# A hybrid trunk's FFN gate and up tiles by seven half-depth products instead of eight

## The chip, the cores and the metric

One program on one core of one Trainium2 chip. The metric is the time of one execution on the device in microseconds (us), lower is better. All arithmetic is fp32: each product is made of fp32 operands split in two parts for TensorE.

## The reference

Two layers are applied to 640 tokens of 1024 features: 128 tokens of a context stream and 512 of a sample stream, with the same weights and two different modulation vectors (shift, scale, gate). Each layer is an FFN, a token mixing and a second FFN:

```python
def swiglu(h, w_in, w_out):
    gate, up = jnp.split(h @ w_in, 2, axis=-1)
    return (jax.nn.silu(gate) * up) @ w_out
...
    mod = (jax.nn.silu(cond) @ lp['w_mod'] + lp['b_mod'])[:, None, :]
...
    x = x + 0.5 * g1 * swiglu(modulate(rmsnorm(x, nw[0]), sh1, sc1), lp['ffn_w_in'][0], lp['ffn_w_out'][0])
    y, s_ssd, s_ret, k, v = token_mixing(modulate(rmsnorm(x, nw[1]), sh2, sc2), lp, ssd_s0, ret_s0, ctx_kv)
    x = x + g2 * y
    x = x + 0.5 * g3 * swiglu(modulate(rmsnorm(x, nw[2]), sh3, sc3), lp['ffn_w_in'][1], lp['ffn_w_out'][1])
```

w_in is 1024 x 5632 (2816 gate columns, 2816 up columns), w_out 2816 x 1024, both different for each of the four FFNs. The token mixing projects to four groups of heads (state space, Hyena with long convolutions whose filters come from a small network, retention, attention) and back.

## The kernel before

Everything is feature-major: a tensor holds 128 features on the partitions and tokens along the columns. x is eight such tiles of 640 tokens, worked on in two groups of 320 columns (group 0 has the 128 context tokens and 192 of the sample's). A matmul takes a 128x128 piece of weights and 320 columns of activations; every product of weights w and activations h is three matmuls, w_hi*h_hi, w_hi*h_lo and w_lo*h_hi (`mm3`, lines 326 to 332), accumulated in PSUM.

*Weights.* `wload` (L317) loads up to 128x1024 into `raw` (two buffers, RB), ACT copies it to `hi`, DVE makes `lo` = raw - hi (L61). *Activations.* `norm` (L303) squares x on ACT, adds the squares over the feature tiles on POOL (`nsum`, L282; on DVE at the very start), sums over partitions by matmuls, takes the power -0.5 on POOL (`nrs`, L120), spreads the result by another matmul, scales x on DVE (`nx`, L70) and splits it into `hh` (ACT) and `hl` (DVE, 640 columns at a time). The shifts stand as two extra columns beside group 0 (`shifts`, L297), so that the products of group 0 have 322 columns and bring what the shifts add.

*FFN* (`ffn`, L348, four times). The 22 pairs of gate and up tiles of 128 columns each (a pair is called a gate/up tile, or a tile, below) run in chunks of 6, 5, 4, 4 and 3; after each chunk its part of the down projection is accumulated into x (`accumulate`, L342). For a pair, each group and each matrix is a product over eight depth tiles:

```python
 355              for ci, nk in enumerate(FFN_CHUNKS):
 356                  G = []
 357                  for f in range(ff, ff + nk):
 358                      wg, wu = (ahead[i] if 2 * f + i < len(ahead) else self.wload(I["ffnin"][li, w, 2 * f + i], 1024)
 359                                for i in range(2))
 360                      gh = self.ring("gh", 640, F32R)
 361                      gl = self.ring("gl", 640, F32R)
 362                      for g in range(2):
 363                          c = slice(320 * g, 320 * g + 320)
 364                          pg = self.unit(wg, g)
 365                          if g == 0:
 366                              cg = mp.tile([128, 2, 2], F32, tag="cg", name="cg", bufs=3)
 367                              self.ccopy(cg[:, 0], pg[:, 320:322])
 368                          t = mp.tile([128, 320], F32, tag="sg", name="sg", bufs=3)
 369                          for a, b, st in GCOLS[g]:
 370                              self.act(t[:, a:b], pg[:, a:b], AF.Silu, bias=cg[:, 0, st : st + 1])
 371                          pu = self.unit(wu, g)
 372                          if g == 0:
 373                              self.ccopy(cg[:, 1], pu[:, 320:322])
 374                          p = mp.tile([128, 320], F32, tag="gu", name="gu")
 375                          for a, b, st in GCOLS[g]:
 376                              self.stt(p[:, a:b], pu[:, a:b], cg[:, 1, st : st + 1], t[:, a:b], ADD, MUL)
 377                          self.acopy(gh[:, c], p)
 378                          self.tt(gl[:, c], p, gh[:, c].bitcast(F32), SUB)
 379                          credit += 2.0 if ci == 0 else rate
 380                          while credit >= 1.0:
 381                              next(mods, None)
 382                              credit -= 1.0
 383                      G.append([(gh[:, 320 * g : 320 * g + 320], gl[:, 320 * g : 320 * g + 320]) for g in range(2)])
```

`mods` are pieces of the modulation that later stages need, computed inside the FFNs: each piece reduces one 128x1024 weight tile against silu(cond) on DVE (`wmj`, L270). `credit` pulls four pieces per pair in the first chunk, then `rate` x 2 per pair (rates 1.5, 1, 1, 1), and one per output tile of the down projection. The four FFNs have 96, 64, 80 and 16 pieces to do.

*Order.* The program is written as above, and the framework's scheduler makes each engine's queue from it by its own estimates; an engine takes its queue in that order. Pieces of the modulation are pinned to the program's order. The Hyena filters of a layer (`filters`, L442; small matmuls with names mx, w, h, pm, tab_c) are written ahead of an FFN (the first and the third feed-forward) and mixed by the scheduler into its first matmuls. The names: mm is a product's PSUM tile, mx any other PSUM tile; PSUM has eight banks, three for mm and five for mx. `ring` buffers (NB = 22 of 128x640) hold x, the gate-times-up tiles `gh` and `gl` of a chunk, and the mixers' inputs.

In the trace the FFNs run from 52 to 540, 950 to 1450, 1462 to 1930 and 2340 to 2814 us; the mixers lie between the first and second, and the third and fourth.

## Time and profile before

| | |
|---|---|
| median of two runs | 2812.73 us (2810.97 and 2814.49) |
| the profiled execution: its time, its span | 2814.49 us, 2814.5 us |
| PE busy | 2751.3 us, 98% of the span, 18,470 instructions |
| DVE busy | 1678.3 us, 60% |
| ACT busy | 915.1 us, 33% |
| POOL busy | 123.7 us, 4% |

PE is TensorE, DVE VectorE, ACT ScalarE, POOL GpSimd. The granted clock of PE is given for a stretch as a share of its full speed. In time order a row gives the start, the length and, in brackets, the idle time before it with what ended it.

### The profile page before, as it was taken

To read this page: it belongs to the slowest core of one execution; us is meant where nothing else is said; L and a number is where in the kernel's file an instruction comes from. 1 tells how busy PE (TensorE), PEld (TensorE's weight loads), DVE (VectorE), ACT (ScalarE), POOL (GpSimd) and SP (SyncE) were. 2 spreads that over 40 slices of the span, in tenths; PEclk is the share of its full clock that TensorE was granted. 3 is DMA by queue.
4 is the path that set the end of the run, shared out by engine and by line. 5 is a ranking of instruction groups with operands and counts; after the bars stand their busy time and mean duration, and the time that the engine had idled before them with its cause. 6 is when DMAs were issued, how large, how long until landed. Compare 5 with 4: busy or idle time off the path is not lost.

```text
span 2814.5 us, 46104 instructions
## 1 busy us (share of the span) xinstructions
PE 2751.3 (98%) x18470; PEld 2661.3 (95%) x18470; DVE 1678.3 (60%) x3658; ACT 915.1 (33%) x1952; POOL 123.7 (4%) x201
## 2 busy tenths in 40 slices
PE   6999999999999999999999999999999999999999
PEld 4899999999999789999989999998999998999999
DVE  6685666566756767555457655656558577433433
ACT  3222222333555322222233222223245534222222
POOL 0000000200010200000020000002001012000000
PEclk9999999999999999999999999999999999999999
DMA  6353444322211244334214433443222123222222
GB/s 239 126 181 119 141 144 130 134 79 62 90 58 55 96 153 160 103 122 135 75 59 147 133 100 117 134 139 102 68 80 80 57 69 128 76 74 77 76 69 89
DMA packets 118289, 300.74 MB, mean 107 GB/s; under 512 B 19614, under 2 KB 42222, under 8 KB 117564
## 3 DMA queue, kind: packets, MB, share of 16 engines
q1 hardware_dynamic: 118076, 297.80, 33.3%
q8 instruction: 146, 2.39, 0.3%
q14 instruction: 67, 0.55, 0.1%
HBM read 283.55 MB, written 14.20 MB: 106 GB/s over the span
## 4 chain that ended last, share of the span: by engine, by line
PE 92%; DVE 3%; POOL 1%; DMA 1%; issue 1%; ACT 1%; SPq 0%; POOLq 0%; ACTq 0%; DVEq 0%
PE mm L88 81%; PE mx L88 10%; PE mx L93 2%; POOL nsum L282 1%; DVE nx L70 1%; DVE hl L61 0%; POOL nrs L120 0%; DVE x L70 0%; DVE lo L61 0%; DMA E<-cumd 0%; DMA wms<-in_wmod 0%; POOL arr L120 0%; ACT nsq L73 0%; DVE ndg L61 0%; DVE wmj L270 0%
## 5 line engine op out<-in xcount | busy, mean ns | idle before, releaser
L88 PE MATMUL mm<-hh,lo 128*128 128x320 f32 (+2 forms) x3936 | 1234.9, 314 | 4.9 <-DVE lo L61 4.9
L88 PE MATMUL mm<-hh,hi 128*128 128x320 f32 (+2 forms) x3936 | 1235.7, 314 | 2.8 <-ACT hi L76 1.4
L88 PE MATMUL mm<-hl,hi 128*128 128x320 f32 (+2 forms) x3936 | 1231.1, 313 | 4.3 <-DVE hl L61 4.3
L88 PEld LDWEIGHTS mm<-hl,hi 128*128 128x128 f32 (+1 forms) x3936 | 745.1, 189 | 15.1 <-issue 6.3
L88 PEld LDWEIGHTS mm<-hh,hi 128*128 128x128 f32 (+1 forms) x3936 | 745.5, 189 | 9.2 <-ACT hh L76 2.7
L88 PEld LDWEIGHTS mm<-hh,lo 128*128 128x128 f32 (+1 forms) x3936 | 742.6, 189 | 11.9 <-DVE lo L61 5.8
L76 ACT CAST hi<-raw 128x1024 fp32r<-128x1024 f32 (+3 forms) x390 | 359.7, 922 | 855.8 <-PE mm L88 813.9
L61 DVE TENSOR_TENSOR lo<-raw,hi 128x1024 fp32r<-128x1024 f32 (+3 forms) x390 | 415.2, 1065 | 234.0 <-ACT hi L76 233.2
L88 PE MATMUL mm<-gl,hi 128*128 128x320 f32 x1408 | 436.3, 310 | 0.0
L88 PE MATMUL mm<-gh,hi 128*128 128x320 f32 x1408 | 436.2, 310 | 0.0
L88 PE MATMUL mm<-gh,lo 128*128 128x320 f32 x1408 | 435.8, 310 | 0.0
L70 DVE SCALAR_TENSOR_TENSOR gu<-mm,cg,sg 128x128 f32<-128x128 f32 (+2 forms) x264 | 108.9, 437 | 410.3 <-ACT cg L76 286.2
L70 DVE SCALAR_TENSOR_TENSOR x<-mm,gate,x 128x128 f32<-128x128 f32 (+2 forms) x576 | 235.9, 435 | 189.9 <-PE mm L88 187.4
L270 DVE CUSTOM_DVE_ANT_0 wmj<-wm,condb 128x1024 bf16<-128x1024 f32 x264 | 321.6, 1218 | 11.4 <-DMA wm<-in_wmodT 6.1
L88 PEld LDWEIGHTS mm<-gl,hi 128*128 128x128 f32 x1408 | 265.4, 189 | 2.1 <-issue 2.1
L88 PEld LDWEIGHTS mm<-gh,hi 128*128 128x128 f32 x1408 | 265.5, 189 | 0.0
L88 PEld LDWEIGHTS mm<-gh,lo 128*128 128x128 f32 x1408 | 265.4, 189 | 0.0
L76 ACT COPY cg<-mm 128x2 f32<-128x2 f32 x176 | 28.0, 160 | 419.6 <-PE mm L88 419.4
L61 DVE TENSOR_TENSOR gl<-gu,gh 128x320 fp32r<-128x320 f32 x176 | 86.1, 489 | 41.8 <-ACT gh L76 41.8
L76 ACT CAST gh<-gu 128x320 fp32r<-128x320 f32 x176 | 80.8, 459 | 91.4 <-DVE gu L70 90.5
L73 ACT ACTIVATE sg<-mm,cg 128x128 f32<-128x128 f32 (+2 forms) x264 | 106.0, 436 | 2.8
L282 POOL TENSOR_TENSOR nsum<-nsum,nsq 128x320 f32<-128x320 f32 x70 | 64.5, 922 | 605.7 <-ACT nsq L73 603.5
(237 smaller groups left out, 1842.2 us busy)
## 6 DMA issues: line engine op xcount, KB each, us to landing
raw<-in_ffnin SPq DMA_DIRECT2D x176, 512.0 KB
wm<-in_wmodT SPq DMA_DIRECT2D x132, 512.0 KB
raw<-in_mixin SPq DMA_DIRECT2D x52, 512.0 KB
raw<-in_ffnoutA SPq DMA_DIRECT2D x64, 256.0 KB
raw<-in_ffnoutA SPq DMA_DIRECT2D x32, 384.0 KB
raw<-in_ffnoutA SPq DMA_DIRECT2D x32, 320.0 KB
wms<-in_wmod SPq DMA_DIRECT2D x12, 512.0 KB
raw<-in_ffnoutB SPq DMA_DIRECT2D x12, 512.0 KB
```

The lines of the kernel that those rows point to most:

```text
L61: self.nc.vector.tensor_tensor(out, a, b, op=op)
L70: self.nc.vector.scalar_tensor_tensor(out, a, s, b, op0=op0, op1=op1)
L73: self.nc.scalar.activation(out, in_, f, **k)
L76: self.nc.scalar.copy(out, in_)
L88: return self.nc.tensor.matmul(out, lhsT=lhsT, rhs=rhs, start=start, stop=stop)
L93: self.nc.tensor.transpose(out, in_, self.ident[b : b + n, b : b + n])
L270: return self.nc.vector.tensor_tensor_reduce(junk, raw, cb, 1.0, 0.0, op0=MUL, op1=ADD, accum_out=out)
L282: adder.tensor_tensor(s, s, sq, op=ADD)
```

## The change

Let A be the 2x2 blocks of weights of a pair (gate and up, each cut at half the depth: a11 and a12 of gate, a21 and a22 of up, 128x512 each) and B the 2x2 blocks of activations (depth halves by token groups). Instead of the eight block products, seven are made, after Strassen and Winograd: four of them from sums of weight blocks (`sa`, `sb`: four additions of 128x512 per pair, on POOL) and, for the activations, from sums of token blocks (factors T1 to T4, made once per FFN in `sums`, by DVE and ACT: `hr`, `hq`, split in `HX` for T1, and `th`/`tl` for T3, T2 and T4). Products that share a result accumulate in one PSUM tile; partial results are copied to SBUF by ACT (`cp`) and added by DVE.

```diff
-FFN_CHUNKS = (6, 5, 4, 4, 3)
+FFN_CHUNKS = (4, 4, 4, 4, 3, 3)
...
+    def normed(self, li, n, g, j, pb):
+        t = self.ring("hb").rearrange("p (a b) -> p a b", a=2)
+        for i in range(2):
+            m = j + 4 * i
+            self.tt(t[:, i], self.x[m][g], pb, MUL)
+            for a, b, st in GCOLS[g]:
+                self.act(t[:, i, a:b], t[:, i, a:b], AF.Identity, scale=self.sc[li][:, n, m, st : st + 1],
+                         bias=self.mod[li][:, 24 * n + m, st : st + 1])
+        return t
...
+    def norm(self, li, n, g, adder=None, pin=False):
+        pb = self.norm_stats(g, adder or self.nc.gpsimd, pin)
+        yield
+        kept = []
+        for j in range(4):
+            t = self.normed(li, n, g, j, pb)
+            if g == 0:
+                self.split(self.H0[0][:, j], self.H0[1][:, j], t)
+            else:
+                if n == 1:
+                    self.split(self.HX[0][:, j], self.HX[1][:, j], t[:, 0])
+                self.split(self.H3[0][:, j], self.H3[1][:, j], t[:, 1])
+                if n != 1:
+                    kept.append(t)
+                    if not pin:
+                        self.sums(j, t)
+        if pin and g:
+            yield
+            for j in range(4):
+                self.sums(j, kept[j])
+    def sums(self, j, t):
+        b = lambda p, i: self.H0[p][:, j, i].bitcast(F32)
+        q = self.ring("hq").rearrange("p (a b) -> p a b", a=2)
+        r = self.ring("hr").rearrange("p (a b) -> p a b", a=2)
+        self.tt(r[:, 0], t[:, 0], b(0, 0), SUB)
+        self.tt(r[:, 0], r[:, 0], b(1, 0), SUB)
+        self.tt(q[:, 0], t[:, 0], t[:, 1], SUB)
+        self.split(self.HX[0][:, j], self.HX[1][:, j], r[:, 0])
+        self.tt(q[:, 1], t[:, 1], r[:, 0], SUB)
+        self.split(self.T[0][:, j, 0:2], self.T[1][:, j, 0:2], q)
+        self.tt(r[:, 1], b(0, 1), q[:, 1], SUB)
+        self.tt(r[:, 1], r[:, 1], b(1, 1), ADD)
+        self.split(self.T[0][:, j, 2], self.T[1][:, j, 2], r[:, 1])
...
+    def product(self, ps, w, half, which, first, last):
+        for j, (h, l) in enumerate(self.factor(which)):
+            c = slice(512 * half + 128 * j, 512 * half + 128 * j + 128)
+            k = {} if first else {"skip_group_check": True}
+            self.mm(ps, w[0][:, c], h, start=first and j == 0, stop=False, **k)
+            self.mm(ps, w[0][:, c], l, start=False, stop=False, **k)
+            self.mm(ps, w[1][:, c], h, start=False, stop=j == 3, **k)
...
+    def quad(self, li, w, f, sp, mp, halves, ahead=None):
+        nc = self.nc
+        gate, up = ahead or (self.rawload(self.I["ffnin"][li, w, 2 * f + i], 1024) for i in range(2))
+        a11, a12, a21, a22 = gate[:, :512], gate[:, 512:], up[:, :512], up[:, 512:]
+        sa = sp.tile([128, 2, 512], F32, tag="sa", name="sa", bufs=1)
+        sb = sp.tile([128, 2, 512], F32, tag="sb", name="sb", bufs=SB)
+        add = lambda o, a, b, op: nc.gpsimd.tensor_tensor(o, a, b, op=op)
+        ab = self.wsplit(gate)
+        add(sa[:, 0], a21, a11, SUB)
+        add(sb[:, 0], a21, a22, ADD)
+        add(sa[:, 1], sb[:, 0], a11, SUB)
+        add(sb[:, 1], a12, sa[:, 1], SUB)
+        new = lambda pool, tag, name: pool.tile([128, 512], F32, tag=tag, name=name)[:, :320]
+        A, B, C = new(self.mmp, "mm", "mm"), new(self.xtp, "xt", "mb"), new(self.xtp, "xt", "mc")
+        sg = mp.tile([128, 640], F32, tag="sg", name="sg", bufs=2)
+        gu = mp.tile([128, 640], F32, tag="gu", name="gu", bufs=2)
+        def copied(ps, name):
+            t = mp.tile([128, 320], F32, tag="cp", name=name, bufs=3)
+            self.acopy(t, ps)
+            return t
+        self.product(B, ab, 1, "B21", True, True)
+        self.product(A, ab, 0, "B11", True, False)
+        p1 = copied(A, "p1")
+        self.tt(sg[:, :320], B, p1, ADD)
+        self.act(sg[:, :320], sg[:, :320], AF.Silu)
+        wa = self.wsplit(sa.rearrange("p a b -> p (a b)"))
+        self.product(C, wa, 0, "T3", True, False)
+        p7 = copied(C, "p7")
+        yield
+        w4 = self.wsplit(a22)
+        self.product(A, wa, 1, "T2", False, False)
+        q = copied(A, "q")
+        self.product(C, w4, 0, "T4", False, True)
+        self.tt(gu[:, :320], C, q, ADD)
+        self.tt(gu[:, :320], gu[:, :320], sg[:, :320], MUL)
+        gh = self.ring("gh", 640, F32R)
+        gl = self.ring("gl", 640, F32R)
+        if halves:
+            self.split(gh[:, :320], gl[:, :320], gu[:, :320])
+        yield
+        wb = self.wsplit(sb.rearrange("p a b -> p (a b)"))
+        self.product(A, wb, 0, "T1", False, False)
+        self.tt(gu[:, 320:], A, p7, ADD)
+        yield
+        self.product(A, wb, 1, "B22", False, True)
+        self.act(sg[:, 320:], A, AF.Silu)
+        self.tt(gu[:, 320:], gu[:, 320:], sg[:, 320:], MUL)
+        o = 320 if halves else 0
+        self.split(gh[:, o:], gl[:, o:], gu[:, o:])
+        self.G.append([(gh[:, 320 * g : 320 * g + 320], gl[:, 320 * g : 320 * g + 320]) for g in range(2)])
...
+            ends = [sum(FFN_CHUNKS[: i + 1]) for i in range(len(FFN_CHUNKS))]
+            prev = None
+            for f in range(22):
+                q = self.quad(li, w, f, sp, mp, f == 21, ahead if f == 0 else None)
+                next(q)
+                if prev is not None:
+                    next(prev)
+                next(q)
+                if prev is not None:
+                    finish(prev)
+                    if f in ends:
+                        ci = ends.index(f)
+                        down(f - FFN_CHUNKS[ci], FFN_CHUNKS[ci])
+                prev = q
+                credit += 4.0 if f < FFN_CHUNKS[0] else 2.0 * rate
+                while credit >= 1.0:
+                    next(mods, None)
+                    credit -= 1.0
...
-NB = 22
+NB = 18
-RB = 2
+RB = 3
```

Also in the diff:
- `wload` is cut into `rawload` (DMA) and `wsplit` (the split in hi and lo), so that POOL can read `raw`; RB goes from 2 to 3.
- The shifts are added by ACT in `normed` (scale and bias of an Identity), with DVE's product x times the root ahead of it into a ring buffer `hb`; the extra columns 320 and 321 and what read them (`cg`) are gone, every product has 320 columns.
- PSUM: three banks mm, two xt (for `mb` and `mc` of the pairs; in the mixers two of each five mx tiles), three mx.
- At an FFN's entry each of the four quarters of the second group is split, then combined with the first group's at once; at the first FFN all combining stands behind both norms. The filters are written behind it.
- Chunk by chunk the down projection comes one pair later: the last two products of a pair stand behind the first three of the next one.
- The mixers' constant tables (`setup_mix`) are loaded in each mixer into a pool of its own instead of once; NB goes from 22 to 18, and the buffers of the modulation's weights at the start from 6 and 4 to 5 and 3.

Where the first feed-forward begins, PE's queue has the end of the filters like this before (mm: the products of the first pair, of both groups; mx with pm, w: the filters):

```order
L88 MATMUL mm<-hh_103,lo 128x322
L88 MATMUL mm<-hh_104,hi 128x320
L88 MATMUL mm<-hl_106,hi 128x320
L88 MATMUL mm<-hh_104,lo 128x320
L88 MATMUL mx<-pm_669,tab_c 128x256
L88 MATMUL mx<-pm_670,tab_c 128x256
L88 MATMUL mx<-w_684,h_655 128x512
L88 MATMUL mm<-hh_104,hi 128x320
L88 MATMUL mm<-hl_106,hi 128x320
L88 MATMUL mm<-hh_104,lo 128x320
```

and like this after (mc and mm with th, tl: products of the combined activations T3 and T2, behind the pair's first two products):

```order
L82 MATMUL mx<-w_739,h_727 128x512
L82 MATMUL mx<-pm_741,tab_c 128x256
L82 MATMUL mx<-pm_742,tab_c 128x256
L82 MATMUL mx<-w_756,h_727 128x512
L82 MATMUL mx<-pm_758,tab_c 128x256
L82 MATMUL mx<-pm_759,tab_c 128x256
L82 MATMUL mc<-th,hi 128x320
L82 MATMUL mc<-tl,hi 128x320
L82 MATMUL mm<-th,hi 128x320
L82 MATMUL mm<-tl,hi 128x320
L82 MATMUL mc<-th,lo 128x320
```

Before, the filters' matmuls stand among the products of the first pair; after, the last of them stand in a row ahead of the first product with a combined factor.

At the entry of the third feed-forward DVE's queue, for the second group, has before (ndg spreads the roots, nx and hl are the scaled and split activations, lo weights):

```order
L61 TENSOR_TENSOR ndg<-ident,nrs 64x320
L61 TENSOR_TENSOR lo<-raw,hi 128x1024
L70 SCALAR_TENSOR_TENSOR nx<-x_9149,sc_110,mx 128x320
L70 SCALAR_TENSOR_TENSOR nx<-x_9150,sc_110,mx 128x320
L70 SCALAR_TENSOR_TENSOR nx<-x_9151,sc_110,mx 128x320
L70 SCALAR_TENSOR_TENSOR nx<-x_9152,sc_110,mx 128x320
L61 TENSOR_TENSOR hl_106<-nx,hh_104 128x640
L61 TENSOR_TENSOR lo<-raw,hi 128x1024
L61 TENSOR_TENSOR hl_106<-nx,hh_104 128x640
L70 SCALAR_TENSOR_TENSOR nx<-x_9153,sc_110,mx 128x320
```

and after (hb the scaled x, h3l and hxl splits of the second group and of T1, hq and hr the sums, tl the split of T3, T2 or T4):

```order
L61 TENSOR_TENSOR h3l<-hb,h3h 128x320
L61 TENSOR_TENSOR hxl<-hr,hxh 128x320
L61 TENSOR_TENSOR hq<-hb,hr 128x320
L61 TENSOR_TENSOR hb<-x_9309,mx 128x320
L61 TENSOR_TENSOR hr<-h0h,hq 128x320
L61 TENSOR_TENSOR tl<-hq,th 128x640
L61 TENSOR_TENSOR hr<-hr,h0l 128x320
L61 TENSOR_TENSOR hb<-x_9313,mx 128x320
L61 TENSOR_TENSOR hr<-hb,h0h 128x320
L61 TENSOR_TENSOR tl<-hr,th 128x320
L61 TENSOR_TENSOR hr<-hr,h0l 128x320
```

Where two nx and one hl made two depth tiles ready, the queue now has two hb, six sums or differences and four splits for them.

Inside a pair of the first feed-forward DVE's queue has before (wmj and mod a piece of the modulation, its ISA rows one instruction each with its result):

```order
L61 TENSOR_TENSOR lo<-raw,hi 128x1024
L61 TENSOR_TENSOR mod_107<-mod_107,par_91 128x2
L270 ISA wmj,mod_107<-wm,condb 128x1024
L270 ISA mod_107 128x1
L70 SCALAR_TENSOR_TENSOR gu<-mm,cg,sg 128x320
L270 ISA wmj,mod_107<-wm,condb 128x1024
L270 ISA mod_107 128x1
L61 TENSOR_TENSOR gl<-gu,gh 128x320
L61 TENSOR_TENSOR mod_107<-mod_107,par_91 128x2
L270 ISA wmj,mod_107<-wm,condb 128x1024
L270 ISA mod_107 128x1
```

and after (lo of a whole gate tile, of sa and of sb, and of half an up tile; sg and gu are sums fed from PSUM and the silu products):

```order
L61 TENSOR_TENSOR lo<-raw,hi 128x1024
L61 TENSOR_TENSOR mod_112<-mod_112,par_94 128x2
L61 TENSOR_TENSOR gu<-mc,q 128x320
L61 TENSOR_TENSOR lo<-sa,hi 128x1024
L61 TENSOR_TENSOR gu<-gu,sg 128x320
L61 TENSOR_TENSOR lo<-sb,hi 128x1024
L61 TENSOR_TENSOR gu<-gu,sg 128x320
L61 TENSOR_TENSOR gl<-gu,gh 128x640
L275 ISA wmj,mod_112<-wm,condb 128x1024
L275 ISA mod_112 128x1
L61 TENSOR_TENSOR sg<-mb,p_1233 128x320
L275 ISA wmj,mod_112<-wm,condb 128x1024
```

A pair's two lo of 1024 columns have become three and one of 512, `gl` is split once for both groups, and five sums and products stand where three gu stood. POOL's queue, empty in the pairs before, has four additions for each pair, here the last pair of the first FFN, followed by the squares' sums of the next norm:

```order
L427 TENSOR_TENSOR sa<-raw 128x512
L427 TENSOR_TENSOR sb<-raw 128x512
L427 TENSOR_TENSOR sa<-sb,raw 128x512
L427 TENSOR_TENSOR sb<-raw,sa 128x512
L287 TENSOR_TENSOR nsum<-nsum,nsq 128x320 x7
```

raw are the blocks of gate and up. A pair's weights go from DMA over POOL, ACT and DVE to PE now, where they went over ACT and DVE.

## Rows read from the trace of the kernel before

**Rows 1.** The page's head: span, busy us of each engine (share) and instructions.
```profile
span 2814.5 us, 46104 instructions
...
PE 2751.3 (98%) x18470; PEld 2661.3 (95%) x18470; DVE 1678.3 (60%) x3658; ACT 915.1 (33%) x1952; POOL 123.7 (4%) x201
```

**Rows 2.** Stretches inside two feed-forwards: busy us (instructions) by engine, clock, DMA.
```profile
core 0: us, PE busy (x) PEld busy (x) DVE busy (x) ACT busy (x) POOL busy (x), PEclk, DMA share, GB/s
1300.00:1400.00 100.00, 100.00 (x680) 100.00 (x679) 40.99 (x76) 28.48 (x53) 0.00 (x0) 1.00 0.33 104
2500.00:2600.00 100.00, 100.00 (x680) 100.00 (x679) 37.32 (x65) 25.66 (x51) 0.00 (x0) 1.00 0.26 78
```

**Rows 3.** DVE in time order, first feed-forward: start us, length us, instruction.
```profile
154.91 1.22 DVE L61 TENSOR_TENSOR lo<-raw,hi 128x1024 fp32r<-128x1024 f32 x1
156.05 0.15 DVE L61 TENSOR_TENSOR mod<-mod,par 128x2 f32<-128x2 f32 x1
156.12 1.22 DVE L270 CUSTOM_DVE_ANT_0 wmj<-wm,condb 128x1024 bf16<-128x1024 f32 x1
157.26 0.55 DVE L70 SCALAR_TENSOR_TENSOR gu<-mm,cg,sg 128x320 f32<-128x320 f32 x1
157.72 1.22 DVE L270 CUSTOM_DVE_ANT_0 wmj<-wm,condb 128x1024 bf16<-128x1024 f32 x1
```

**Rows 4.** Groups: DVE's lo (busy us, mean ns), POOL's nsum (ns min/median/max).
```profile
L61 DVE TENSOR_TENSOR lo<-raw,hi 128x512 fp32r<-128x512 f32 x64 | 43.9, 687 | 11.8 <-ACT hi L76 11.8
...
L282 POOL TENSOR_TENSOR nsum<-nsum,nsq x70: 857/877/1735, 535.0 to 2337.3; 128x320 f32<-128x320 f32 x70
```

**Rows 5.** DVE and POOL in time order at places where they meet or stand alone.
```profile
22.65 1.21 DVE L270 CUSTOM_DVE_ANT_0 wmj<-wm,condb 128x1024 bf16<-128x1024 f32 x1
22.88 2.02 POOL L120 TENSOR_TENSOR nrs<-rsq,mhalf 64x5 f32<-64x5 f32 x1 [21.17 <-DVE rsq L67]
...
964.15 0.81 DVE L61 TENSOR_TENSOR hl<-nx,hh 128x640 fp32r<-128x640 f32 x1
...
1447.98 1.17 POOL L120 TENSOR_TENSOR nrs<-rsq,mhalf 64x5 f32<-64x5 f32 x1 [1.07 <-DVE rsq L67]
...
1460.64 1.24 DVE L70 SCALAR_TENSOR_TENSOR nx<-x,sc,mx 128x192 f32<-128x192 f32 x4
1460.71 1.80 POOL L282 TENSOR_TENSOR nsum<-nsum,nsq 128x320 f32<-128x320 f32 x2 [0.43 <-ACT nsq L73]
1461.93 1.26 DVE L61 TENSOR_TENSOR hl<-nx,hh 128x640 fp32r<-128x640 f32 x1
...
1463.51 1.21 DVE L61 TENSOR_TENSOR lo<-raw,hi 128x1024 fp32r<-128x1024 f32 x1
1463.67 2.82 POOL L120 TENSOR_TENSOR nrs<-rsq,mhalf 64x5 f32<-64x5 f32 x1 [1.16 <-DVE rsq L67]
1464.64 0.81 DVE L61 TENSOR_TENSOR hl<-nx,hh 128x640 fp32r<-128x640 f32 x1
```

**Rows 6.** PE in time order where the third feed-forward begins; idle before it in brackets.
```profile
1462.56 0.74 PE L88 MATMUL mx<-ones,nsum 128*64 128x1 f32 x10 [1.88 <-POOL nsum L282]
1464.77 0.64 PE L88 MATMUL mm<-hh,lo 128*128 128x322 f32 x1 [1.47 <-DVE lo L61]
1465.21 0.47 PE L88 MATMUL mm<-hh,hi 128*128 128x322 f32 x1
1465.48 0.47 PE L88 MATMUL mm<-hl,hi 128*128 128x322 f32 x1
```

**Rows 7.** The two stretches with the filters: instructions on the mm tiles alone.
```profile
core 0: us, PE busy (x) PEld busy (x) DVE busy (x) ACT busy (x), PEclk, DMA share, GB/s
64.00:123.00 59.00, 33.55 (x203) 30.27 (x202) 2.52 (x6) 3.15 (x10) 1.00 0.33 100
961.00:1025.00 64.00, 38.07 (x221) 34.77 (x222) 3.35 (x8) 3.93 (x14) 0.97 0.28 85
```

231 lines of the change are left out of this document (110 added, 121 removed).

## The prediction

> **What bounds the kernel now.** I read the page's head first, then the table by stretches, then the time order of DVE and POOL, because the change moves work from the first engine to the other two. The span is 2814.5 us and PE is busy in 2751.3 us of it [rows 1]; all its idle time together is 63 us. In the feed-forward stages PE runs without a hole: 680 matmuls start in each 100 us at a granted clock of 1.00, its 2.4 GHz level, which is 147 ns per matmul of 320 columns, while DVE is busy 37 to 41% in these stretches, which have no modulation pieces left, and POOL not at all [rows 2]. So a matmul less is 147 ns less, as long as DVE, ACT and POOL still deliver the operands in time. That condition carries the forecast.
>
> **Term 1, the matmuls.** A gate/up tile has 2 matrices x 2 token groups x 8 depth tiles x 3 = 96 matmuls before and 7 products x 4 half-depth tiles x 3 = 84 after. 22 tiles x 4 feed-forwards x 12 = 1056 fewer (the program's mm, mb and mc matmuls number 15,936 before and 14,880 after, the same difference: the change does what it says). 1056 x 147 ns = 155 us. The first group also loses its two shift columns, 322 to 320: 2/320 of 147 ns is 0.9 ns, on about 5,500 matmuls 5 us. Together -160 us. For 84 matmuls PE now needs 12.35 us per tile, where it took 14.1.
>
> **Term 2, DVE and POOL inside a tile.** Starts in time order give what one DVE instruction occupies: lo of 1024 from 154.91 to 156.05, 1.14 us; a modulation piece (wmj) 1.14, with its half of the small add 1.18; an operation fed from PSUM on 320 columns 0.46 [rows 3]. Lengths overlap the next start by 0.08, so lo of 512 (0.69 long) occupies 0.6 and hl on 640 (0.81) 0.74 [rows 4, 5]; by the line through 640 and 1024 an operation of 320 occupies 0.4. A tile after the change has 3 lo of 1024 (gate, sa, sb), one of 512, one gl of 640, three PSUM-fed sums and two products of silu: 3 x 1.14 + 0.6 + 0.74 + 3 x 0.46 + 2 x 0.40 = 6.9 us. On top come the pieces that the loop pulls: 4 per tile in the first four tiles of each feed-forward (16 tiles), 3 in tiles 4 to 18 of the first one (15), 2 in tiles 4 to 15 of the second and 4 to 18 of the third (27), none in 30. That is 11.6, 10.4, 9.3 and 6.9 us of DVE against 12.35 of PE: DVE alone would still fit.
>
> POOL's four adds of 512 columns per tile do not come free. An add of 320 takes 857 ns at best, 877 in the median [rows 4]; by columns 512 take at most 1.4 us, I take 1.3 and 5.2 per tile. And they exclude DVE work with two SBUF inputs. A POOL add next to PSUM-fed nx keeps 0.86 us, but hl that starts under it takes 1.26 instead of 0.81; the tiny nrs takes 1.17 alone, 2.02 when it starts under a wmj, and 2.82 when it starts under lo and hl comes directly behind [rows 5]. So lo, gl, the products and wmj all stand against POOL, and only the three PSUM-fed operations (1.4 us) run beside it. Packed without loss a tile needs DVE + 5.2 - 1.4: 15.4, 14.2, 13.1, 10.7 us. Over 12.35 that is 3.05 x 16 + 1.85 x 15 + 0.75 x 27 = 97 us. If each add blocks DVE fully (1.3 less the 0.1 of DVE's start that overlaps, 4.8 per tile) it is 16.4, 15.2, 14.1, 11.7: 4.05 x 16 + 2.85 x 15 + 1.75 x 27 = 155 us. The lower bound is 0: the adds fall into DVE's own waits. I take +115, near the packed value, since DVE has some waits for PE.
>
> The last case of rows 5 also says who pays. nrs did not get in between lo and hl: back-to-back DVE instructions kept POOL out. The Trainium skill (SBUF — State Buffer, Who interferes with whom) says instead that the second to issue "fully blocks" until the first finishes, which would have let nrs in before hl. By that rule DVE pays at once, the 155 us; by the row POOL starves until DVE meets a PSUM-fed operation, and DVE pays when lo of sa has no sa. The Trainium skill (GPSIMD Engine Reference, Performance versus the Vector engine) gives 4497 ns for an add of 2048 columns; by it 512 would be an estimated 1.12 us, and term 2 some 40 us smaller.
>
> **Term 3, the entries.** T3, T2 and T4 need the second group's normed tokens combined with the first's, so in the first tile PE has 24 matmuls (3.5 us) before it needs all sums. Per quarter DVE does 6 operations of 320 (0.4), three subtractions of 320 and one of 640: 4.4 us, 17.6 in all, with the eight hb 3.5 more, and every chain goes to ACT and back: some 25 us. Before, the 48 matmuls of the first group covered that time, and the stall at this place was 1.9 + 1.5 us [rows 6]. So an entry costs 25 - 3.5 - 3 = 18.5, plus about 2 because the matmuls behind such a stall start 0.27 us apart for some us [rows 6]: 20 us. At two of the four entries the filters stand behind the sums on DVE and, by the new order, ahead of T3 on PE. Before, in 59 and 64 us around the filters 203 and 221 product matmuls ran between [rows 7], 29.8 and 32.5 us of work. After, only 24 stand ahead: 31 - 3.5 = 27 lost, plus most of the sums' 18.5, less some 8 because DVE's other work of that stretch (lo, gu) is no longer in the chain: 38 us. 2 x 38 + 2 x 20 = +116 us. Bounds: 50 (chains overlap well) and 160 (the filters' own matmuls at the lower clock).
>
> **Term 4, restarts.** After each of five down-projection blocks per feed-forward the next tile's two raw weights queue behind the eight down weights in a ring of three, then wait for POOL's adds. The down block is short of covering this by about nothing or by a few us: 20 x 0.75 = +15, bounds 0 and 60. While it runs, DVE needs about 2.9 us per output tile (0.6 + some 1.1 of accumulates, from 0.46 per 320 columns and one start more, + 1.18) against 24 x 147 ns = 3.53, so it does not bind.
>
> **Smaller edits at nothing.** ACT gets one and a half more casts and three more copies per tile; it was busy 26 to 28% of such a stretch [rows 2] and stays under 60%; if that cover goes, a tile slows by tenths of a us. The mixer has 18 instead of 22 ring buffers and reloads its tables: its stages hide both unless conv units are held back; -5 to +30 us.
>
> **Sum.** 2814.5 - 160 + 115 + 116 + 15 = 2900 us. The profiled execution's span is within 2 us of the median of the two runs, 2812.7, so nothing is added for that.
>
> **Rivals.**
> *A, the adds are hidden* (25%). One mechanism decides: whether POOL finds its 5.2 us per tile in DVE's waits and PSUM-fed operations. Term 2 is then 0 and the time 2814.5 - 160 + 116 + 15 = 2785 us, not slower. For it: DVE needs 6.9 to 11.6 us of 12.35 per tile, so 0.75 to 5.4 us are free in every tile. Against: free and PSUM-fed time together are 2.2, 3.4 and 4.5 us in the 58 tiles with pieces, under 5.2; it decides from where POOL has worked ahead in the down blocks.
> *B, the entries are cheap as well* (14%): the sums flow quarter by quarter into T3, and the filters' chain, freed from other DVE work, is much shorter. Entries 50, terms 2 and 4 near 0: 2705 us, faster. Against: PE takes its queue in order, and the order puts every filter matmul ahead of T3.
> *C, the restarts bind* (14%): raw tiles, adds, cast and lo follow one another behind each down block, and the accumulates that free PSUM stand behind that lo on DVE. At 5 us a restart: 20 x 5 = 100 instead of 15, 2985 us. For it: the three-buffer ring; against: 24 matmuls of the new tile need the gate half alone.
>
> **How the numbers follow.** The forecast case, 2870 to 2960, has 47%. About 2% either way is what a measurement here tells from no change (2756 to 2869). Faster is B, 0.14; same is A with a part of B's and the forecast's edges, 0.26; slower is the forecast and C, 0.60. The range must reach down over A to the edge of B and up into C: 2755 to 2990. The forecast's own range is 2860 to 2960.
>
> **What would show it.** Right: 100 us stretches with mean starts over 165 ns in the first feed-forward and near 147 to 155 in the last tiles of the fourth; lo and wmj with means well above the 1.22 us of rows 3, or long DVE waits for the lo of sa; POOL adds between 1.3 and 2.5 us; PE idle for 20 us or more at each entry, over 35 where the filters are. Term 1 is wrong if the matmuls start more than 147 ns apart while nothing is waited for. The forecast falls if PE stays busy above 95% inside the tiles, or if entries cost PE under 10 us.

## The result and the profile after

The changed kernel takes 3097.14 us (median of 3093.94 and 3100.33), 1.1009 of the time before, interval [1.0977, 1.1042]: slower, as forecast, but by 284 us where 87 were forecast and above the range. The page's head (answers to [rows 1]):

```profile
span 3098.3 us, 45587 instructions
...
PE 2752.3 (89%) x17414; PEld 2570.0 (83%) x17414; DVE 2212.0 (71%) x4152; ACT 1137.9 (37%) x2174; POOL 724.0 (23%) x553
```

PE has 1056 instructions less and the same busy time: what it gained in number it lost in length, since it ran some stretches at or near the lower clock (the entries, below). Stretches inside the first and the fourth feed-forward (columns as in [rows 2]):

```profile
400.00:500.00 100.00, 89.62 (x593) 86.64 (x592) 87.99 (x141) 32.32 (x51) 30.25 (x16) 1.00 0.39 124
2860.00:2960.00 100.00, 98.56 (x662) 96.94 (x661) 59.83 (x93) 38.80 (x63) 24.86 (x16) 1.00 0.25 77
```

Where pieces of the modulation and weight additions meet (first row), 593 matmuls start in 100 us where 680 did; in the fourth feed-forward, without pieces, 662 do. The stretches by stage, cut where the last accumulate of a stage into x ends (first FFN, mixer, second FFN, third FFN, mixer, fourth FFN):

```profile
0.00:647.10 647.10, 532.53 (x3168) 479.31 (x3168) 505.39 (x867) 221.95 (x383) 168.11 (x112) 0.94 0.39 128
647.10:1067.00 419.90, 399.71 (x2689) 370.46 (x2689) 259.38 (x684) 163.09 (x409) 38.02 (x69) 0.96 0.23 75
1067.00:1658.50 591.50, 500.92 (x3026) 464.62 (x3026) 438.88 (x726) 207.51 (x350) 173.23 (x110) 0.91 0.30 98
1658.50:2181.60 523.10, 462.29 (x2928) 444.73 (x2928) 427.13 (x691) 195.59 (x326) 164.73 (x100) 0.94 0.34 112
2181.60:2609.50 427.90, 407.84 (x2689) 377.42 (x2689) 259.46 (x685) 166.07 (x411) 39.53 (x69) 0.94 0.22 73
2609.50:3095.50 486.00, 449.00 (x2914) 433.52 (x2914) 321.77 (x506) 183.64 (x304) 140.34 (x93) 0.95 0.25 80
```

Cut the same way, the stages of before are 555.8, 394.4, 510.5, 481.3, 393.7 and 476.0 us. So the FFNs lost 91, 81, 42 and 10 us, the mixers 25.5 and 34.2. For the terms of the forecast I took PE's starts in time order and, in each stretch, the time beyond 0.1472 us per product matmul (100 us for the 680 of [rows 2] are 0.147), after minus before. An entry is the time up to the 168th product matmul of an FFN (in the kernel before, where filters stand, up to the last filter matmul); a restart is a pair that begins behind a down block; the rest of an FFN is the second row.

| term | forecast | found |
|---|---|---|
| 1, matmuls | -160 | -156 |
| 2, pairs and down blocks | +115 | +124 (pairs some 84, down blocks some 40) |
| 3, entries: the two with filters | +76 | +137 (66, 71) |
| 3, entries: the two without | +40 | +56 (24, 31) |
| 4, restarts | +15 | +63 (25, 14, 23, 1) |
| mixers | 0 | +60 |
| sum | +86 | +284 |

**The ports.** All engines in time order at the third down block of the first feed-forward:

```profile
329.50 2.08 DVE L275 CUSTOM_DVE_ANT_0 wmj<-wm,condb 128x1024 bf16<-128x1024 f32 x1
...
330.47 2.27 POOL L427 TENSOR_TENSOR sb<-raw 128x512 f32<-128x512 f32 x1
...
331.52 2.30 DVE L61 TENSOR_TENSOR lo<-raw,hi 128x1024 fp32r<-128x1024 f32 x1
...
332.81 2.13 POOL L427 TENSOR_TENSOR sa<-sb,raw 128x512 f32<-128x512 f32 x1
...
333.74 1.22 DVE L61 TENSOR_TENSOR mod<-mod,par 128x2 f32<-128x2 f32 x1
...
336.23 0.86 DVE L70 SCALAR_TENSOR_TENSOR x<-mm,gate,x 128x192 f32<-128x192 f32 x2
...
336.78 0.38 PE L82 MATMUL mm<-gh,hi 128*128 128x320 f32 x1 [2.49 <-DVE x L70]
...
337.58 0.47 PE L82 MATMUL mm<-gh,lo 128*128 128x320 f32 x1
...
337.85 0.47 PE L82 MATMUL mm<-gh,hi 128*128 128x320 f32 x1
```

wmj takes 2.08 us and lo 2.30 instead of 1.22 [rows 3], an addition 2.1 to 2.3 instead of the 1.26 that it takes alone (below), and a sum of two columns 1.22 instead of 0.15. The two engines take turns, and each instruction's time has in it the rest of the other engine's. The accumulates (x, L70) stand behind this on DVE, PE waits 2.49 us for one, and the matmuls behind the wait start 0.27 us apart instead of 0.147. Inside the pairs what PE waits for most is lo, the split of sa (for T3) and of half an up tile (for T4), as the page's row of these matmuls shows:

```profile
L82 PE MATMUL mc<-th,lo 128*128 128x320 f32 x704 | 227.8, 324 | 61.9 <-DVE lo L61 61.8
```

**An entry with filters.** The filters stand at the first and the second feed-forward ([rows 7], 64 and 961 us), not at the first and the third, as the part on the kernel before has it. POOL, ACT and PE in time order, first feed-forward, and PE's stretches at the four entries (columns as in [rows 2]):

```profile
52.95 0.52 POOL L595 MEMSET h<- 1x512 f32 x1 [13.38 <-PE mx L82]
...
115.03 0.20 POOL L595 MEMSET h<- 1x128 f32 x1 [61.42 <-PE mx L82]
...
131.38 1.26 POOL L427 TENSOR_TENSOR sa<-raw 128x512 f32<-128x512 f32 x1 [16.00 <-DVE kout L70]
132.60 1.26 POOL L427 TENSOR_TENSOR sb<-raw 128x512 f32<-128x512 f32 x1
...
135.29 1.33 POOL L427 TENSOR_TENSOR sb<-raw,sa 128x512 f32<-128x512 f32 x1
```

```profile
143.73 0.60 ACT L73 ACTIVATE kco<-mx 128x512 f32<-128x512 f32 x1 [4.92 <-PE mx L82]
144.22 0.42 ACT L76 COPY p<-mm 128x320 f32<-128x320 f32 x1
...
145.57 1.03 ACT L76 CAST hi<-sa 128x1024 fp32r<-128x1024 f32 x1
```

```profile
62.51 1.97 PE L82 MATMUL mx<-feats,w 33*64 33x512 f32 x2
...
66.97 0.47 PE L82 MATMUL mm<-h0h,lo 128*128 128x320 f32 x1
83.28 1.96 PE L82 MATMUL mx<-h,w 64*64 64x512 f32 x2 [15.84 <-ACT h L73]
...
141.59 2.05 PE L82 MATMUL mx<-pm,tab_c 128*128 128x256 f32 x4 [1.71 <-DVE pm L61]
146.65 0.63 PE L82 MATMUL mc<-th,hi 128*128 128x320 f32 x1 [3.01 <-ACT hi L76]
```

```profile
68.00:146.00 78.00, 41.89 (x98) 23.67 (x98) 46.18 (x103) 11.31 (x25) 5.37 (x6) 0.65 0.14 40
1080.00:1173.00 93.00, 47.19 (x110) 26.13 (x109) 58.56 (x130) 22.45 (x43) 5.36 (x6) 0.59 0.15 44
1662.00:1694.00 32.00, 17.24 (x55) 12.11 (x53) 24.76 (x50) 15.51 (x29) 11.76 (x9) 0.50 0.10 34
2612.00:2668.00 56.00, 32.05 (x137) 24.72 (x137) 46.47 (x74) 26.47 (x51) 23.11 (x16) 0.63 0.12 40
```

PE has 24 products, then 80 us of filters alone (66.97 to 146.65), then T3. The first addition waits for kout, a buffer of the filters that its own has nothing to do with; presumably sa takes memory that the filters held. But that wait is not the one that ends last: the additions are done at 136.6 us, while PE has filter matmuls in its queue until 143.6, and ACT takes the pair's copy p and the cast of sa only behind kco, the filters' last copy.

The filters' own chain is longer as well. From their first matmul to the end of their last it takes 81 us, and 87 in the second feed-forward, where it took 58 and 64 before. Some 13 and 15 us of that lie between feats and the next layer (the wait of 15.84 us), where DVE makes the sums before it turns to the filters; the other 9 and 8 follow at a lower clock. The granted clock of the two stretches is 0.65 and 0.59, nearer the lower level (1.2 GHz, 0.5) than the upper one, where the stretches of [rows 7] had 1.00 and 0.97 with product matmuls between. The entry without filters (third row) runs at 0.50, wholly at that level. There the sums are what is waited for, one quarter of the depth after the other, as PE in time order shows:

```profile
1684.23 0.64 PE L82 MATMUL mc<-th,hi 128*128 128x320 f32 x1 [2.94 <-ACT th L76]
1689.46 0.64 PE L82 MATMUL mc<-th,hi 128*128 128x320 f32 x1 [2.94 <-ACT th L76]
```

### The profile page after: what moved, and what is told of

Same layout as the page of the kernel before. It is cut to its first block, busy times and chain, and to the rows that moved or that the text cites. A ratio compares the mean times of both kernels' runs of the same rounds, so it can differ in the third digit from the quotient of the medians.

```text
span 3098.3 us, 45587 instructions
## 1 busy us (share of the span) xinstructions
PE 2752.3 (89%) x17414; PEld 2570.0 (83%) x17414; DVE 2212.0 (71%) x4152; ACT 1137.9 (37%) x2174; POOL 724.0 (23%) x553
## 5 line engine op out<-in xcount | busy, mean ns | idle before, releaser
L76 ACT CAST hi<-raw 128x512 fp32r<-128x512 f32 (+3 forms) x422 | 327.5, 777 | 683.5 <-PE mm L82 608.2
L61 DVE TENSOR_TENSOR lo<-raw,hi 128x512 fp32r<-128x512 f32 (+3 forms) x422 | 440.2, 1044 | 190.2 <-ACT hi L76 189.7
L70 DVE SCALAR_TENSOR_TENSOR x<-mm,gate,x 128x128 f32<-128x128 f32 (+2 forms) x672 | 271.0, 434 | 192.2 <-PE mm L82 190.7
L82 PE MATMUL mm<-h0h,hi 128*128 128x320 f32 (+1 forms) x912 | 291.0, 319 | 12.0 <-ACT hi L76 10.0
L82 PE MATMUL mm<-h0h,lo 128*128 128x320 f32 (+1 forms) x912 | 290.6, 319 | 2.5 <-DVE lo L61 2.5
L82 PE MATMUL mm<-h0l,hi 128*128 128x320 f32 (+1 forms) x912 | 291.4, 320 | 0.0
L82 PE MATMUL mc<-th,lo 128*128 128x320 f32 x704 | 227.8, 324 | 61.9 <-DVE lo L61 61.8
L82 PE MATMUL mc<-th,hi 128*128 128x320 f32 x704 | 224.8, 319 | 33.9 <-ACT th L76 20.9
L82 PE MATMUL mc<-tl,hi 128*128 128x320 f32 x704 | 224.2, 318 | 0.4 <-DVE tl L61 0.3
L82 PE MATMUL mm<-h3h,hi 128*128 128x320 f32 (+1 forms) x632 | 203.8, 322 | 14.3 <-DVE gu L61 14.1
L82 PE MATMUL mm<-h3l,hi 128*128 128x320 f32 (+1 forms) x632 | 200.3, 317 | 0.0
```

The lines of the kernel that those rows point to most:

```text
L61: self.nc.vector.tensor_tensor(out, a, b, op=op)
L70: self.nc.vector.scalar_tensor_tensor(out, a, s, b, op0=op0, op1=op1)
L76: self.nc.scalar.copy(out, in_)
L82: return self.nc.tensor.matmul(out, lhsT=lhsT, rhs=rhs, start=start, stop=stop, **k)
```

## The experiments

Times without an interval are single runs; the kernel before took 2814 to 2817 us beside them.

### The weight additions

**no_adds**

```diff
-        add(sa[:, 0], a21, a11, SUB)
-        add(sb[:, 0], a21, a22, ADD)
-        add(sa[:, 1], sb[:, 0], a11, SUB)
-        add(sb[:, 1], a12, sa[:, 1], SUB)
...
+            for t in self.sab:
+                nc.gpsimd.memset(t, 0.01)
+        sa, sb = self.sab
```

> The changed kernel with the four weight additions of every pair left out: sa and sb are constant buffers, filled once per FFN, their splits on ACT and DVE and all products stay as they are. Theory P (DVE and GpSimd exclude one another on two-input instructions, so an addition is paid by both): the loss inside the pairs of the first three feed-forwards (1.5 to 4 us a pair, 4 to 7 us behind a down block in the trace of after, some 190 us in all with the fourth) shrinks to what DVE's own load leaves, and wmj falls from a mean of 1.49 us to 1.22: 2930 to 2990 us. Rival L (the time goes because the chain from a raw tile to the products has one link more and too few buffers; the ports do not matter): wmj and lo keep their lengths, but the chain is shorter here too; time 2990 to 3060. Rival D (DVE has too much work of its own with pieces, sums and splits): 3060 to 3097.

2908.6 us, 188 less than the changed kernel and even below what theory P gave. Without additions a restart loses 0.0 to 0.1 us and a pair outside the first ones nothing. That the 188 equal terms 2 and 4 of the table (124 + 63) is chance: by stretches the pairs give back their 84 us, the restarts 63 and the entries 35 (13, 13, 3 and 7), but the down blocks only 7 of 40. wmj is back at a mean of 1.216 us. DVE's own load is not what binds: in the stretch from 400 to 500 us it is busy 85 us and PE 99, 673 matmuls starting.

```profile
400.00:500.00 100.00, 99.28 (x673) 98.55 (x672) 85.10 (x161) 39.95 (x65) 0.00 (x0) 1.00 0.44 140
```

**adds_dve**

```diff
-        add = lambda o, a, b, op: nc.gpsimd.tensor_tensor(o, a, b, op=op)
+        add = self.tt
```

> The same additions on DVE instead of GpSimd, result unchanged. Theory P: an addition of 512 columns occupies DVE for 0.6 us, so 2.4 us a pair, less than the four lockouts cost (some 4 us); wmj back at 1.22 us; the loss in the pairs of the first three feed-forwards falls to about half: 2980 to 3050 us. Rival L: the link stays, only on another engine and shorter: 3050 to 3090. Rival D (DVE's own load binds): each pair gets 2.4 us more on the engine that binds, 58 pairs: 3150 to 3240, slower than the changed kernel.

2978.7 us, 1.0592 [1.0566, 1.0618] of before and 118 us faster than the changed kernel, though DVE has 352 instructions more: just under theory P's range (2980 to 3050). The chain from raw tile over additions, cast and lo is still there, yet the restarts lose 0 to 2 us instead of up to 7. The groups of wmj, in the changed kernel and here (busy us, mean ns):

```profile
L275 DVE CUSTOM_DVE_ANT_0 wmj<-wm,condb 128x1024 bf16<-128x1024 f32 x264 | 393.1, 1489 | 0.1
```

```profile
L275 DVE CUSTOM_DVE_ANT_0 wmj<-wm,condb 128x1024 bf16<-128x1024 f32 x264 | 320.9, 1215 | 0.0
L61 DVE TENSOR_TENSOR sb<-raw,sa 128x512 f32<-128x512 f32 x88 | 60.4, 687 | 1.2
```

An addition of 512 columns is 0.69 us on DVE; on POOL the four groups of the changed kernel have means of 1.45 to 1.85 us. The entries with filters stay as they were (86 and 100 us beyond the matmuls up to the second pair, 88 and 102 in the changed kernel), so neither POOL nor its memset ahead of the additions was what held them.

**short_pieces**

```diff
-        return self.nc.vector.tensor_tensor_reduce(junk, raw, cb, 1.0, 0.0, op0=MUL, op1=ADD, accum_out=out)
+        return self.nc.vector.tensor_tensor_reduce(junk[:, :16], raw[:, :16], cb[:, :16], 1.0, 0.0, op0=MUL, op1=ADD, accum_out=out)
```

> The changed kernel with each modulation piece cut to 16 of 1024 columns (the part of the sum over the other columns is left out), its transfer and its place in the queue kept. Theory P: the pieces are what meets the additions on DVE, so the first three feed-forwards come near the fourth, which loses nothing in its pairs and 1.5 us at a down block: 2900 to 2970 us. Rival L: pairs still wait for raw tile, addition and cast, 3050 to 3090. Rival D: like P, but GpSimd's additions keep the lengths of 1.4 to 2.1 us that they have in the first feed-forward; under P they fall to 1.4 to 1.6.

2958.5 us, within P's range. The additions' means fall to 1.41 to 1.55 us (P), but not to 1.26. The additions, the ring, the casts and the splits are all there, and the restarts lose 0.0 to 0.8 us. It takes both, additions and pieces, for most of the loss: either one away brings 139 to 188 us.

### The entries

**filt3**

```diff
-FPOS = (0, 0)
+FPOS = (3, 3)
```

> The changed kernel with the filters of a layer built in its mixer, behind the convolution units' inputs, instead of ahead of its first FFN. Theory E (at the two entries with filters the first additions wait for memory that the filters' buffers held and stand behind the filters' memset in GpSimd's queue, so that all filters run ahead of the first product with a combined factor, alone on PE and at its lower clock): the two entries fall from 88 and 102 us lost to the 26 to 39 of the other two, and the filters cost some 25 to 35 us each in the mixers: 3010 to 3050 us. Rival F (the filters' own chain costs this wherever it stands): 3080 to 3110. Rival S (the token sums at the entry are what PE waits for there): the entries stay above 70 us.

3013.2 us, 1.0696 [1.0678, 1.0714] of before, 84 us faster than the changed kernel, as theory E had it: the filters ahead of T3 are what costs. The first two FFNs are 70 and 68 us shorter, the mixers with the filters 27 and 28 us longer. It does not tell the filters' memory from the place that they have in the queues.

**plain1**

```diff
+                if f < 1:
+                    self.plain(li, w, f, mp, ahead if f == 0 else None)
+                    if f == 1 - 1:
+                        for j in range(4):
+                            self.sums(j, self.kept[j])
...
```

> The changed kernel with the first pair of each FFN as eight products (96 matmuls), the token sums written behind it; result unchanged, 48 matmuls (7 us) more in all. Theory E (at the entries with filters the memory of the filters' buffers is what is waited for; at the other two it is the sums): the entries without filters, 26 and 39 us lost, fall to 10 to 15 each; those with filters, 88 and 102, gain 5 to 15 each, since PE finds 48 matmuls more before a buffer of the FFN is needed: 3030 to 3070 us. Rival S (the sums hold PE at all four): those with filters fall by 35 us or more each: 2960 to 3010 us.

3063.4 us, 1.0877 [1.083, 1.0923] of before. The first two FFNs, with the filters, gained some 15 us each, so S falls. In the first of them PE still has no product from 74 to 131 us, in the middle of a pair that needs no addition and no sum: it is the filters' turn, and the additions are not what holds PE there. But E's other half missed: the third FFN became 2 us shorter, the fourth 6. In the third PE then waits 7.4 us ahead of the third pair, for `sg` of the second, which stands behind the sums on DVE; the sums had only been moved.

**no_sums**

```diff
-                    if not pin:
-                        self.sums(j, t)
...
-        return [[self.T[p][:, j, ("T3", "T2", "T4").index(which)] for p in range(2)] for j in range(4)]
+        return [[self.H0[p][:, j, ("T3", "T2", "T4").index(which) % 2] for p in range(2)] for j in range(4)]
```

> The changed kernel with the token sums left out: T1 to T4 are replaced by split token blocks that stand there anyway, so DVE and ACT make at an entry only the 16 scaled tiles and their splits. Theory T (the sums' chain of some 25 us is what PE waits for at the two entries without filters): the first two pairs of the third and fourth feed-forward, 30 and 39 us lost, fall to 10 to 15 each; at the entries with filters, 94 and 109, where the filters bind, by less than 15 each: 3020 to 3060 us. Rival U (what is waited for is the longer norm, scale and shift on ACT between DVE's product and the split): the entries keep 25 us or more: 3075 to 3100 us.

3032.1 us: each FFN is 13 to 17 us shorter, so the sums cost some 60 us in all. In the third FFN the time beyond the matmuls up to the 168th falls from 34 to 21 us, in the fourth from 40 to 26, above the 15 of theory T and about the 25 of U: both are true in part. Some 3 and 7 us more of these two entries went in no_adds; the 10 or so that are left above the 9 and 8 us of before I put down to the norm's longer chain, which no run took away at these two places. Where the filters stand (15 and 17 us) the sums cost by standing ahead of the filters on DVE: in the first feed-forward PE's wait of 15.84 us for the filters' second layer falls to 5.54, and T3 starts 12.3 us sooner, still behind the last filter matmul.

### The mixers

**before_ring**, the kernel before with

```diff
-FFN_CHUNKS = (6, 5, 4, 4, 3)
+FFN_CHUNKS = (4, 4, 4, 4, 3, 3)
-NB = 22
+NB = 18
```

> The kernel before with two settings of the changed one: 18 ring buffers instead of 22 and chunks of 4, 4, 4, 4, 3, 3. Theory N (the changed mixers are 25 and 34 us longer because the ring is shorter and holds units back): the two mixers become 20 us or more longer here too, 2850 to 2880 us in all. Rival Q (the mixers lose at their ends, by the longer norms, and to the clock behind those waits): mixers within 8 us of before, 2810 to 2835 us in all.

2824.7 us, mixers 395.3 and 393.6: the ring and the chunks cost the mixers nothing (N falls) and the first feed-forward some 10 us.

**before_layout**, the same with

```diff
+        self.xtp = pool("xtp", 2, space=PSUM)
-        self.mxp = pool("mxp", 5, space=PSUM)
+        self.mxp = pool("mxp", 3, space=PSUM)
...
+        with self.tc.tile_pool(name="mixc", bufs=1, side="left", reuse_waits="tile") as p:
+            self.setup_mix(p)
```

> The kernel before with all that the change does to memory outside the FFN: 18 ring buffers, chunks of 4, 4, 4, 4, 3, 3, the mixers' tables loaded in each mixer, and PSUM as three, two and three banks, two of which the mixers share. Theory M (tables and banks cost the changed mixers their 25 and 34 us): mixers 15 us or more longer than before's 394 and 394; 2855 to 2890 us. Rival Q (norms and the clock behind their waits): mixers within 5 us; 2820 to 2840 us.

2858.8 us, mixers 414.8 and 407.7: 20 and 14 us longer with all products as before. Theory M, the second mixer just under its bound.

**before_tables**, before_layout without the pools of PSUM.

> The run before_layout without its PSUM edit: 18 ring buffers, the other chunks, tables loaded in each mixer, but five banks in one pool as before. Theory M1 (the tables: a mixer's pool of its own and its loads cost what before_layout showed, 20 and 14 us): mixers 410 to 416 and 405 to 410 us, 2840 to 2860 in all. Theory M2 (the banks: only three for the filters, the norms and the rest outside the mixers, and a fixed turn between two pools inside): mixers within 5 us of 395, and the entries of the first two feed-forwards as in before_ring: 2820 to 2835 us.

2824.9 us: theory M2. It was the banks: 20 and 10 us. The mixers' stretches of the two kernels, before_layout and before_tables:

```profile
562.10:976.90 414.80, 397.01 (x2687) 370.08 (x2687) 260.42 (x688) 169.62 (x433) 35.10 (x64) 0.97 0.24 77
1968.50:2376.20 407.70, 396.70 (x2687) 369.42 (x2687) 259.63 (x688) 168.57 (x432) 34.20 (x64) 0.97 0.21 68
```

```profile
561.00:955.50 394.50, 383.24 (x2687) 361.47 (x2687) 260.08 (x688) 171.74 (x435) 32.71 (x64) 0.99 0.26 81
1944.90:2342.30 397.40, 387.04 (x2687) 364.57 (x2687) 260.26 (x688) 170.34 (x434) 32.83 (x65) 0.98 0.23 70
```

With the same instructions PE is busy 14 and 10 us longer at a lower mean clock, and idle 6.5 and 0.6 us longer.

**norm1**

```diff
...
+                        self.stt(t[:, i, a:b], self.x[m][g][:, a:b], self.sc[li][:, n, m, st : st + 1], pb[:, a:b], MUL, MUL)
+                        self.act(hi[:, a:b], t[:, i, a:b], AF.Identity, bias=s)
+                        self.stt(lo[:, a:b], t[:, i, a:b], s, hi[:, a:b].bitcast(F32), ADD, SUB)
```

> The changed kernel with the norm ahead of each mixer made otherwise, result unchanged: DVE scales, ACT adds the shift in the same instruction that makes hi, DVE makes lo from both, so ACT has one pass less between DVE's two. Rival Q of the mixers: their first products start 4 to 7 us sooner, the mixers are 5 to 12 us shorter each: 3070 to 3090 us. Theory M: mixers unchanged: 3090 to 3105 us.

3085.9 us, in Q's range by the sum, but the mixers are only 4.4 and 3.3 us shorter where 5 to 12 were expected: the longer norm is a small part, if any, for the first FFN, which the edit leaves alone, is 3.1 us shorter too.

**onepool**

```diff
-        self.xtp = pool("xtp", 2, space=PSUM)
-        self.mxp = pool("mxp", 3, space=PSUM)
...
+        self.mxp = pool("mxp", 5, space=PSUM)
...
-        A, B, C = new(self.mmp, "mm", "mm"), new(self.xtp, "xt", "mb"), new(self.xtp, "xt", "mc")
+        A, B, C = new(self.mmp, "mm", "mm"), new(self.mxp, "mx", "mb"), new(self.mxp, "mx", "mc")
```

> The changed kernel with PSUM in two pools of three and five banks, as before: mb and mc of a pair take banks of the five, the mixers all five in turn. Result unchanged. Theory M2 (the split banks cost the mixers 20 and 10 us by before_tables and before_layout): mixers 420 and 428 fall to 398 to 405 and 410 to 418; 3060 to 3080 us in all. Rival (in the changed kernel the mixers lose to norms and clock, the banks matter only where they are the one edit): mixers 415 us or more, 3085 to 3100 us.

3046.2 us, less than theory M2 gave, since the second mixer gained 26 us where 10 to 18 were expected. The mixers are 403.3 and 402.1 us, 17 and 26 less: the banks are 42 of the mixers' 60 us in the changed kernel. The stretches of the two mixers:

```profile
644.90:1048.20 403.30, 387.33 (x2688) 364.40 (x2688) 259.01 (x685) 163.48 (x409) 36.47 (x69) 0.97 0.25 78
2154.50:2556.60 402.10, 385.81 (x2688) 363.28 (x2688) 259.24 (x685) 165.67 (x411) 36.37 (x69) 0.97 0.24 78
```

### All together

**combo_plain1**: additions on DVE, filters in the mixers, the first pair by eight products, and

```diff
-                credit += 4.0 if f < FFN_CHUNKS[0] else 2.0 * rate
+                credit += 4.0 if li == 0 and f < FFN_CHUNKS[0] else 2.0 * rate
...
-TSPLIT = 8, 3, 8
-RATES = 1.5, 1.0, 1.0, 1.0
+TSPLIT = 8, 3, 9
+RATES = 1.1, 0.25, 1.3, 0.0
```

> All together, result unchanged: additions on DVE, filters in the mixers, the first pair of each FFN by eight products with the sums behind it, and the modulation pieces spread (four per pair only in the first chunk of the first two FFNs, rates 1.1, 0.25, 1.3 and 0, none in the fourth FFN). If the losses are separate, as theories P and E have them: 3097 - 118 - 84 (both measured) - 80 (four entries, from 26 to 39 lost to about 12) - 25 (pieces) = 2790 us, 2760 to 2830, about as fast as the kernel before. If they share their time (rival): 2840 to 2900 us.

2880.2 us, 1.0239 [1.0224, 1.0255] of before: the rival's range. The entries had not become cheap (plain1).

**combo_plain2**: `if f < 2`, the sums behind the second pair.

> As the run before, with the first two pairs of each FFN by eight products: 48 matmuls (7 us) more, and 14 us more cover at each entry. If the sums (some 25 us at an entry) still show behind one pair: 2775 to 2800 us and faster than with one pair; if one pair covers them: 7 us slower than with one.

2879.0 us, 1.0229 [1.0203, 1.0256]: neither outcome. The sums began only when the last plain pair was at work, so a second pair covered nothing.

**best2**: as combo_plain2 with onepool and norm1, and

```diff
+                    if f == 0:
+                        rs = [self.sums(j, self.kept[j]) for j in range(4)]
+                    if f == 2 - 1:
+                        for j in range(4):
+                            self.split(self.HX[0][:, j], self.HX[1][:, j], rs[j][:, 0])
```

> All edits that helped, result unchanged: additions on DVE, filters in the mixers, pieces spread, five banks in one pool, the mixers' norm with one pass less on ACT, the first two pairs of each FFN by eight products, and the token sums written between these two pairs with only the split of T1 behind the second (in combo_plain2 all sums began when the second pair was at work). If sums and banks are what is left: 2879 - 20 to 30 (banks) - 8 (norm) - 15 to 20 at each of four entries = 2765 to 2795 us, faster than before. Rival (DVE has no room for the sums beside a pair's own work wherever they stand): 2830 to 2860 us.

2830.3 us, 1.0044 [1.0025, 1.0064]: 49 us less than combo_plain2, and at the rival's lower edge. Of the 49, the mixers have 14 and 21. In the first three FFNs the three pairs behind the first now lose 6 to 15 us together, where they lost 13 to 21.

**best3**: the same with three pairs by eight products.

> As best2 with three pairs by eight products, the sums still behind the first: 7 us of matmuls more. Faster than best2 only if the sums take DVE longer than one pair covers (14 us and 3.5): then 2755 to 2790; else 7 us slower than best2.

2821.6 us, 1.0027 [1.0016, 1.0039], faster than best2 by 9 but above the range given.

**best4**

```diff
-                    next(mods, None)
+                    if nk > 3:
+                        next(mods, None)
...
-                credit += 4.0 if li == 0 and f < FFN_CHUNKS[0] else 2.0 * rate
+                credit += 4.0 if (li == 0 or w == 1) and f < FFN_CHUNKS[0] else 2.0 * rate
...
-TSPLIT = 8, 3, 9
-RATES = 1.1, 0.25, 1.3, 0.0
+TSPLIT = 8, 3, 8
+RATES = 1.35, 0.45, 1.1, 0.0
```

> As best3, with the pieces laid out once more: none in the fifth down block, whose 18 matmuls per output tile (2.65 us) are shorter than DVE's split, accumulates and piece (some 2.9 us), the fourth FFN takes 16 again, four per pair in the first chunk of all but the third, rates 1.35, 0.45, 1.1 and 0. best3 loses 5 to 8 us in the pairs behind that block in each of the first three FFNs. If the pieces make that: 2822 - 12 to 20 + 3 = 2802 to 2812 us, at or just below the kernel before. If it is the block's own accumulates and splits: 2818 to 2826 us.

2811.3 us (2804.4 to 2816.5), 0.9976 [0.9961, 0.9991] of before: as expected, the 5 to 8 us behind the fifth down block are gone in the first three FFNs. It is the only version with seven products below the kernel before, by a quarter of a per cent, which is no difference by the measure of 2%. Its FFNs are 25.5, 35.9, 12.0 and 10.8 us shorter than before's, with 76 seven-product pairs instead of 88 and the filters moved out of two of them; its mixers, with the filters, 38.0 and 41.5 us longer.

## Why the prediction was wrong, point by point

Of the 198 us between the forecast's 86 and the 284 found, the entries with filters make 61, the mixers 60, the restarts 48 and the entries without filters 16.

*Term 1, right.* 1056 matmuls less at 147 ns are 155 us (the table's cuts put four more into it); where nothing disturbs, the fourth FFN's pairs take their 84 x 0.147 = 12.35 us to the tenth.

*Term 2, right in cause; the agreement in size is partly luck.* 115 were forecast for the pairs. Of the 124 found only some 84 lie in pairs. The first pairs of each FFN stand in the entries, where no_adds brought 35 us more, so the additions cost the pairs some 119 us in all. The other 40 lie in the down blocks, which the forecast put at nothing, and only 7 of them go with the additions; what makes the rest was not followed. That POOL and DVE exclude one another on two-input instructions is shown by no_adds, adds_dve and short_pieces together. One step of the reasoning was wrong: from nrs in [rows 5] it took that DVE's back-to-back instructions keep POOL out until a PSUM-fed one comes. In the trace of after POOL gets in between wmj and lo, and both wait. The Trainium skill (SBUF — State Buffer, Who interferes with whom) says that the one that comes second is blocked for the other's whole instruction, by which DVE pays at once. The 1.22 us of a sum of two columns agrees with it; nrs of [rows 5], which waited for two, stays the exception.

*Term 3, wrong for the entries with filters.* 38 us were forecast for each: 27 for the product matmuls that no longer stand between the filters, then most of the sums' 18.5, less 8 because DVE's other work would leave the chain. Found were 66 and 71. The 27 came as they were read. The step that failed is the rest: the stretch of the filters was to grow by some 10 us and grew by 23, since their chain stands behind the sums on DVE (13 and 15 us) and then takes 9 and 8 us more at a lower clock, which only the upper bound had. In the first feed-forward T3 starts 3 us after them, 8 us more are lost behind T3 up to the 168th product, and the first product comes 5 us later: 27 + 23 + 3 + 8 + 5 = 66. What puts the pair's copy p, the cast of sa and T3 behind the whole of the filters stays open between the memory that the FFN's buffers take over and the order that the scheduler gave; the forecast had read that order rightly. The sums were sized nearly right: 13 to 17 us an FFN in no_sums, 18.5 forecast. The entries without filters are 24 and 31 us instead of 20: sums 12 and 14, additions 3 and 7, and some 10 that I put down to the norm with its one pass more on ACT (argued, not tried).

*Term 4, the place right, the size wrong.* 0.75 us a restart were forecast. Found were 3 to 7 at the first four of the first three FFNs (at one of these twelve nothing), 1 to 2 at their fifth, and nothing to speak of in the fourth FFN, which has no pieces there. Rival C had 5 us, but by the ring of raw tiles and the restart's chain; short_pieces has ring, additions, casts and splits and loses 0.0 to 0.8, and adds_dve, with the chain on DVE, 0 to 2. It is the port again: in the down block above wmj and lo take nearly twice their time and a sum of two columns eight times, and the accumulates stand behind them. The forecast had costed DVE there at 2.9 us per output tile of 3.53, without the additions of the next two pairs, which POOL makes just then. For the two chunks of three pairs it overlooked that an output tile has 18 matmuls, 2.65 us, less than the 2.9; with pieces left out there, best4 won back the 5 to 8 us behind the fifth block.

*The mixers, a step that was missing.* -5 to +30 us were given for ring and tables, and these cost nothing; the banks, which the part on the change names, were not costed at all. They are 42 of 60 us.

*The range.* The upper ends of all terms make 2814.5 - 160 + 155 + 160 + 60 + 30 = 3060 us. What lies above it is term 3 (193 against 160) and the mixers (60 against 30); term 2 stayed 31 us under its bound.

*The rivals.* A and B fell: additions, entries and restarts all cost what they were given or more. The signs named for the forecast came: 593 starts in 100 us (169 ns) in the first FFN, 662 (151 ns) in the fourth, additions of 1.3 to 2.3 us, PE idle for 36 and 46 us in the stretches above where the filters are, 24 at the fourth. At the third it was 15, under the 20 that were named.
